# Storing two branch results as high and low parts instead of splitting them at the merge

## The chip, the cores and the metric

The kernel runs on one core of one Trainium2 chip. The metric is device time in microseconds (us); lower is better. A core has five engines with queues of their own: TensorE (PE, with a separate row PEld for its weight loads), VectorE (DVE), ScalarE (ACT), GpSimd (POOL) and SyncE (SP). Here SP issues nearly all transfers (DMAs), one after the other, and each engine takes its instructions strictly in the order in which they stand. An instruction that waits holds up what stands behind it on the same engine.

## The reference, cut to what matters

One layer over 2048 positions of width 1024 (all float32). One input projection feeds three branches: forgetting attention (12 heads of 64), a state-space layer with a gated linear unit (GLU), and an attention into 256 memory tokens (4 heads of 128). The three results are projected, weighed with gates, added, and projected out:

```python
y_s5 = jax.nn.gelu(y_s5)
y_s5 = y_s5 * jax.nn.sigmoid(y_s5 @ w_glu[l] + b_glu[l])
y_s5 = y_s5 * jax.nn.silu(gs)
...
y_mem = memory_attention(...)
y_mem = y_mem * jax.nn.silu(gm)
gates = jax.nn.sigmoid(gl + b_merge[l]).reshape(Bn, L, N_BRANCH, D_MODEL)
merged = (gates[:, :, 0] * (y_fox @ w_proj_fox[l])
          + gates[:, :, 1] * (y_s5 @ w_proj_s5[l])
          + gates[:, :, 2] * (y_mem @ w_proj_mem[l]))
x = x + merged @ w_out[l]
return rms_norm(x, g_final)
```

`y_s5` and `y_fox` are 768 wide (6 tiles of 128 channels), `y_mem` 512 (4 tiles).

## The kernel before, in words

**High and low parts.** A float32 product is made of three passes in the faster format fp32r (`mm3`): each operand x is split into hi = x rounded to fp32r and lo = x - hi, and PE adds hi·hi, hi·lo and lo·hi. `split` makes the parts of a tile that lies in SBUF: hi on POOL (line 893; on ACT, line 891, once `hi_act` is set, unless `pool=True`), lo on DVE (line 895, or 897 with a scale). Where PSUM is the source, ACT makes hi and DVE lo.

**Stages.** (1) Up to about 1550 us the input projection runs tile by tile on PE, and between its chunks, at fixed rates, the side work: `gen_s5` (to about 930 us), `gen_glu` (to about 1185 us) and `gen_mem` (to about 1535 us). (2) Then the forgetting attention (`gen_fox`) runs, and between its steps a filler: first the rest of the gate projection (`gen_gl`), then `gen_merge0`, the merge of the last quarter of the positions (chunk 3 of 4; a chunk is 512 positions, `CW`). `gen_merge0` begins at about 2350 us, and it has a part 0 (branches 1 and 2, results kept in `s_mp`) and a part 1 (branch 0, added to it). (3) `merge_out` merges chunks 2, 1 and 0 and makes the output projection. All intermediate results go through DRAM (`s["ys"]`, `s["ym"]`, `s["yx"]`, ...).

**What is split where.** `gen_glu` and `gen_mem` store `y_s5` and `y_mem` as plain float32: one store of 256 KB per tile of 128 channels x 512 positions (lines 884 and 678). The merge reads 16 tiles per chunk (`SRC`: six of ys, four of ym, six of yx). `merge_load` loads each into a ring `yr` of two buffers, and splits it into a tile `y` (named `ymg`, 128 x 1024: hi in the left half, lo in the right) with `split(..., pool=True)`, so POOL and DVE each have one instruction per tile.

**In the GLU** each step n loads its gate into `gs` (ring of two), DVE multiplies it into `gt` (line 878), ACT writes the tanh over `gs` (line 882), DVE makes the result in `gs` (line 883), and SP stores it. The load of `gs` two steps on waits until that store has landed.

**What sets the order.** The program is written once in Python order; a scheduler then simulates it and writes a fixed order for every engine. A change of a dependency can so move instructions of other work. The names of tiles in the rows below carry running numbers that differ between the two programs.

**Rings of the merge.** `yp` and `yq` hold 16 `ymg` tiles each. `self.over` is set once the attention is through; the merge then uses PSUM tiles `psA` (3) and `psF` (1) by turns, and `merge_out` uses psB (3) for branch 1, psC (1) for branch 2 and psA for branch 0. In `gen_merge0` the gate tiles `g` and the ring `yr` have two buffers each.

Of the kernel before, what the change touches and what calls it, by code (L numbers as in the profile page):

```python
# [4 lines left out]
F32 = mybir.dt.float32  # L5
F32R = mybir.dt.float32r
# [6 lines left out]
D = 1024  # L13
L = 2048
NC = 4
CW = 512
KD = 8
ML = 256
DF = 768
H = 12  # L20
DH = 64
DM = 512
# [23 lines left out]
def fl32(ap):  # L46
    return ap.bitcast(F32)


class Layer:  # L50
# [17 lines left out]
    def setup(self):  # L68
        nc, i = self.nc, self.i
        self.const, self.close_const = self.pool("const", side="right")  # L70
        self.wp, self.close_wp = self.pool("wp", side="right")
        self.ps, self.close_ps = self.pool("ps", space=PSUM)
        c = self.const
        self.eps = c.tile([128, 1], F32, name="eps")
        nc.vector.memset(self.eps, EPS)
        warm = c.tile([128, 1], F32, name="warm")
        nc.scalar.activation(warm, self.eps, AF.Sqrt)
        self.ident = c.tile([128, 128], F32, name="ident")
        nc.scalar.dma_start(out=self.ident, in_=i["ident"])
        self.g1 = c.tile([128, KD], F32, name="g1")  # L80
        nc.scalar.dma_start(out=self.g1, in_=i["g_norm"])
        self.identb = c.tile([128, 128], BF16, name="identb")
        nc.vector.tensor_copy(self.identb, self.ident)
        pw = self.psC()
        for n in range(WARM):
            nc.tensor.matmul(pw[:, :128], self.identb, self.identb, start=True, stop=True)
        s = {}
        for n, sh, dt in (
            ("qh", [DF, L], F32), ("ql", [DF, L], F32), ("kh", [DF, L], F32), ("kl", [DF, L], F32),
            ("vs", [H, 16, 128, 128], F32), ("gf", [DF, L], F32), ("gs", [DF, L], F32),  # L90
            ("gl", [3 * D, L], F32), ("gm", [DM, L], F32), ("qmh", [DM, L], F32), ("qml", [DM, L], F32),
            ("u", [6, 8, 128, 256], F32), ("kd", [48, 16, 128], F32), ("nf", [H, L], F32), ("yx", [DF, L], F32), ("yc", [6, 8, 128, 256], F32),
            ("ys", [DF, L], F32), ("ym", [DM, L], F32), ("mp", [D, CW], F32), ("mg", [D, L], F32),
            ("mkh", [128, HM, ML], F32), ("mkl", [128, HM, ML], F32),
            ("mvh", [128, 2, DM], F32), ("mvl", [128, 2, DM], F32),
        ):
            s[n] = self.dram("s_" + n, sh, dt)
        self.s = s
# [562 lines left out]
    def mem_pv(self, p, hd, j, G, P):  # L661
        nc, s = self.nc, self.s
        po = self.psC()
        cs = slice(G * 512, (G + 1) * 512)
        for kt in range(2):
            ps = self.psB()
            for b in range(4):
                nc.tensor.transpose(ps[:, b * 128:(b + 1) * 128], P[b][:, kt * 128:(kt + 1) * 128], self.ident)
            hi = p.tile([128, 512], F32R, tag="mhi", name="mhi", bufs=1)
            lo = p.tile([128, 512], F32R, tag="mlo", name="mlo", bufs=1)  # L670
            nc.scalar.copy(hi, ps)
            nc.vector.tensor_sub(lo, ps, fl32(hi))
            vs = slice(j * 128, (j + 1) * 128)
            self.mm3(po, (self.mv[0][:, kt, vs], self.mv[1][:, kt, vs]), (hi, lo), kt == 0, kt == 1)
            yield
        gm = hd[2]
        nc.vector.tensor_mul(gm, po, gm)
        nc.sync.dma_start(out=s["ym"][j * 128:(j + 1) * 128, cs], in_=gm)
        yield

    def gen_mem(self):
# [166 lines left out]
    def gen_glu(self):  # L848
        nc, s = self.nc, self.s
        p, close = self.pool("glu", side="right")  # L850
        t = lambda n, dt=F32, bufs=2: p.tile([128, CW], dt, tag=n, name=n, bufs=bufs)
        for c in range(NC):
            cs = slice(c * CW, (c + 1) * CW)
            ys = []
            for k in range(6):
                y = t("gy")
# [3 lines left out]
                h, l = t(f"gh{k}", F32R, 1), t(f"gl{k}", F32R, 1)  # L860
# [10 lines left out]
            for n in range(6):  # L871
                w = self.load_w(self.i["w_glu"][n], (6, 128))
                r = slice(n * 128, (n + 1) * 128)
                gs = t("gs")
# [6 lines left out]
                    self.mm3(ps, (w[0][:, k, :], w[1][:, k, :]), ys[k], k == 0, k == 5)  # L881
                nc.scalar.activation(gs, ps, AF.Tanh, bias=self.bg[:, n:n + 1], scale=0.5)
                nc.vector.scalar_tensor_tensor(out=gs, in0=gs, scalar=1.0, in1=y, op0=ALU.add, op1=ALU.mult)
                nc.sync.dma_start(out=s["ys"][r, cs], in_=gs)
                yield
        close()

    def split(self, hi, lo, x, sc=1.0, pool=False):
# [7 lines left out]
        else:  # L896
            self.nc.vector.scalar_tensor_tensor(out=lo, in0=x, scalar=sc, in1=fl32(hi), op0=ALU.mult, op1=ALU.subtract)

    SRC = [("ys", k, 1) for k in range(6)] + [("ym", k, 2) for k in range(4)] + [("yx", k, 0) for k in range(6)]

    def merge_load(self, c, part, p, rp, bufs=2):

        for n, k, _ in part:
            raw = rp.tile([128, CW], F32, tag="yr", name="yr", bufs=bufs)
            self.nc.sync.dma_start(out=raw, in_=self.s[n][k * 128:(k + 1) * 128, c * CW:(c + 1) * CW])
            y = p.tile([128, 1024], F32R, tag="y", name="ymg", bufs=16)
            self.split(y[:, :CW], y[:, CW:], raw, pool=True)
            self.ys[c].append((y[:, :CW], y[:, CW:]))

    def merge_gate(self, p, br, m, c, bufs=GB):  # L910
# [254 lines left out]
```

## Time and profile before

| | |
|---|---|
| time, median of 3 runs | 3046.73 us (3043.87 to 3050.66) |
| the profiled execution | 3043.67 us, span 3041.6 us |
| PE busy | 2960.3 us (97%) |
| DVE busy | 1858.7 us (61%) |
| ACT busy | 1015.4 us (33%) |
| POOL busy | 899.2 us (30%) |
| moved by DMA | 417.81 MB, mean 137 GB/s |

The span is the time from the first to the last instruction on the core. The difference between 3043.67 and 3041.6 us lies around it. PE is the engine that is nearly always busy, so time is to be found where PE stands idle or where its clock is granted below full (column PEclk). A row of a view by stretches gives, for each stretch of the span, the busy time of PE, PEld, DVE, ACT and POOL with the number of instructions, then PEclk (1.00 is full), the busy share of the 16 DMA engines and the rate. A row of the waits reads "engine line <- whom it waited for: us in total, times, longest".

### The profile page before, as it was taken

The page shows a single profiled execution, that of the slowest core. Times are in us where ns is not written, and L with a number is a line of the kernel's source. Part 1 is how long each engine was busy: PE and PEld are TensorE (multiplying, and loading weights), DVE is VectorE, ACT ScalarE, POOL GpSimd, SP SyncE. Part 2 cuts the span into 40 slices and gives each one's busy share as a digit, 9 for nine tenths or more (in the row PEclk, how much of TensorE's full clock was granted, in tenths as well). Part 3 has the DMA queues.
Part 4 walks back from the last instruction along what each step waited for, and adds up shares of the span by engine and source line. Part 5 has one row for each costly group of instructions (what it writes and reads, how often), then busy time and mean ns, then how long its engine had stood idle before and what let it go on. Part 6 is the DMA issues. An engine that isn't in the chain of part 4 may idle for free.

```text
span 3041.6 us, 43711 instructions
## 1 busy us (share of the span) xinstructions
PE 2960.3 (97%) x14656; PEld 2424.9 (80%) x14656; DVE 1858.7 (61%) x4982; ACT 1015.4 (33%) x1997; POOL 899.2 (30%) x1212
## 2 busy tenths in 40 slices
PE   8999999999999999999999999999999898999999
PEld 7889977777777778888878888888888676778787
DVE  5332399898986673332217777767777885664444
ACT  5102111111112231222216666666666551212222
POOL 0010000000002332122205666665655764432100
PEclk9999999999999999999999999999999998999999
DMA  5343323323335555344352443444444548777542
GB/s 168 108 136 99 102 87 113 121 88 122 118 128 155 173 158 171 119 122 133 118 165 80 122 120 109 133 118 118 126 117 115 149 130 271 223 226 218 173 145 97
DMA packets 306672, 417.81 MB, mean 137 GB/s; under 512 B 84084, under 2 KB 165236, under 8 KB 306436
## 3 DMA queue, kind: packets, MB, share of 16 engines
q1 hardware_dynamic: 306160, 414.95, 45.8%
q8 instruction: 117, 1.92, 0.3%
q14 instruction: 107, 0.88, 0.1%
q10 hardware_dynamic: 288, 0.07, 0.0%
HBM read 276.00 MB, written 138.90 MB: 136 GB/s over the span
## 4 chain that ended last, share of the span: by engine, by line
PE 80%; DMA 8%; DVE 5%; POOL 3%; issue 3%; ACT 1%; SPq 0%; DVEq 0%; POOLq 0%; ACTq 0%
PE psF L147 10%; PE psF L148 10%; PE psF L149 10%; PE psA L149 8%; PE psA L147 8%; PE psA L148 8%; PE psC L799 5%; PE psB L783 5%; PE psA L751 3%; PE psA L752 3%; PE psC L147 2%; PE psC L149 2%; PE psC L148 2%; DMA wraw<-in_w_out 1%; PE psB L147 1%
## 5 line engine op out<-in xcount | busy, mean ns | idle before, releaser
L147 PE MATMUL psF<-hh,whi 128*128 128x512 f32 (+1 forms) x1160 | 468.9, 404 | 6.2 <-ACT ehi L238 3.1
L149 PE MATMUL psF<-hh,wlo 128*128 128x512 f32 (+1 forms) x1160 | 460.0, 397 | 0.2 <-DVE wlo L895 0.2
L148 PE MATMUL psF<-hl,whi 128*128 128x512 f32 (+1 forms) x1160 | 459.6, 396 | 0.0
L893 POOL TENSOR_SCALAR whi<-wraw 128x1024 fp32r<-128x1024 f32 (+2 forms) x132 | 134.3, 1018 | 703.9 <-PE psA L148 308.0
L895 DVE TENSOR_TENSOR wlo<-wraw,whi 128x1024 fp32r<-128x1024 f32 (+2 forms) x168 | 209.6, 1249 | 190.4 <-POOL whi L893 147.9
L147 PE MATMUL psA<-hh,whi 128*128 128x512 f32 (+1 forms) x816 | 321.8, 396 | 2.9 <-POOL whi L893 1.9
L148 PE MATMUL psA<-hl,whi 128*128 128x512 f32 (+1 forms) x816 | 323.2, 396 | 0.0
L149 PE MATMUL psA<-hh,wlo 128*128 128x512 f32 (+1 forms) x816 | 321.1, 394 | 0.6 <-DVE wlo L895 0.6
L799 PE MATMUL psC<-Pt,v 128*128 128x512 f32 x864 | 267.8, 399 | 7.3 <-DVE Pt L787 4.0
L787 DVE TENSOR_TENSOR Pt<-psB,Pt 128x512 fp32r<-128x512 f32 x336 | 225.5, 684 | 72.9 <-ACT Pt L786 70.7
L147 PEld LDWEIGHTS psF<-hh,whi 128*128 128x128 f32 x1160 | 218.9, 189 | 53.0 <-ACT ehi L238 3.5
L149 PEld LDWEIGHTS psF<-hh,wlo 128*128 128x128 f32 x1160 | 218.8, 189 | 51.5 <-DVE wlo L895 0.6
L148 PEld LDWEIGHTS psF<-hl,whi 128*128 128x128 f32 x1160 | 219.2, 189 | 45.9 <-issue 0.4
L753 DVE CUSTOM_DVE_ANT_0 P<-psA,nf 128x512 f32<-128x512 f32 (+1 forms) x336 | 201.1, 626 | 46.4 <-PE psA L752 27.0
L786 ACT CAST Pt<-psB 128x512 fp32r<-128x512 f32 x336 | 191.6, 586 | 98.8 <-PE psB L783 53.4
L762 POOL TENSOR_SCALAR P<-P,rd 128x768 f32<-128x768 f32 (+1 forms) x240 | 193.8, 823 | 57.4 <-DVE rd L759 34.2
L751 PE MATMUL psA<-kk,qh 128*128 128x512 f32 (+1 forms) x480 | 184.7, 391 | 8.0 <-DVE mx L753 3.9
L147 PEld LDWEIGHTS psA<-hh,whi 128*128 128x128 f32 x816 | 153.6, 189 | 38.3 <-POOL whi L893 2.9
L799 PEld LDWEIGHTS psC<-Pt,v 128*128 128x128 f32 x864 | 154.1, 190 | 35.4 <-DVE Pt L787 7.1
L149 PEld LDWEIGHTS psA<-hh,wlo 128*128 128x128 f32 x816 | 154.0, 189 | 35.5 <-DVE wlo L895 0.8
L783 PE MATMUL psB<-ident,P 128*128 128x128 f32 x1200 | 176.4, 273 | 5.7 <-DVE Pt L787 5.6
L148 PEld LDWEIGHTS psA<-hl,whi 128*128 128x128 f32 x816 | 154.0, 189 | 33.6 <-DVE hl L188 0.2
(372 smaller groups left out, 6259.1 us busy)
## 6 DMA issues: line engine op xcount, KB each, us to landing
wraw<-in_w_in SPq DMA_DIRECT2D x90, 512.0 KB, 4.3
s_gl<-ehi SPq DMA_DIRECT2D x96, 256.0 KB, 2.6
g<-s_gl SPq DMA_DIRECT2D x96, 256.0 KB, 5.0
wraw<-in_w_proj SPq DMA_DIRECT2D x40, 320.0 KB, 4.4
s_vs<-ev_v SPq DMA_DIRECT2D x48, 256.0 KB, 2.7
nf<-s_nf SPq DMA_DIRECT2D x24, 512.0 KB, 6.6
v<-s_vs SPq DMA_DIRECT2D x24, 512.0 KB, 6.8
qh<-s_qh SPq DMA_DIRECT2D x96, 128.0 KB, 3.9
```

Of the source, the lines that this page charges most:

```text
L147: nc.tensor.matmul(out, a[0], b[0], start=first, stop=False)
L148: nc.tensor.matmul(out, a[0], b[1], start=False, stop=False)
L149: nc.tensor.matmul(out, a[1], b[0], start=False, stop=last)
L751: nc.tensor.matmul(ps[:, :wm], q[0][:, qs], kk[:, c0:c0 + wm], start=True, stop=False)
L753: nc.vector.tensor_tensor_reduce(out=pr[:, c * 512:c * 512 + w], in0=ps[:, :w], in1=nf[:, c0:c0 + w], scale=1.0, scalar=-3.0e38, op0=ALU.a ...
L762: nc.gpsimd.tensor_scalar(out=c, in0=c, scalar1=rd, scalar2=0.5, op0=ALU.mult, op1=ALU.mult)
L783: nc.tensor.transpose(ps[:, o:o + 128], P[b][:, kt * 128:(kt + 1) * 128], self.ident)
L786: nc.scalar.copy(hi, psv)
L787: nc.vector.tensor_sub(lo, psv, fl32(hi))
L799: self.pe = nc.tensor.matmul(o, v, m, start=(kt == 0), stop=(kt == 2 * G + 1))
L893: self.nc.gpsimd.tensor_scalar(out=hi, in0=x, scalar1=sc, scalar2=1.0, op0=ALU.mult, op1=ALU.mult)
L895: self.nc.vector.tensor_sub(lo, x, fl32(hi))
```

## The change

`gen_glu` and `gen_mem` split their results where they are made, and store both parts; `merge_load` loads the two parts of ys and ym straight into the halves of the `ymg` tile. The results of the forgetting attention (yx) are stored, loaded and split as before.

```diff
-            ("ys", [DF, L], F32), ("ym", [DM, L], F32), ...
+            ("ysh", [DF, L], F32), ("ysl", [DF, L], F32), ("ymh", [DM, L], F32), ("yml", [DM, L], F32), ...
@@ mem_pv
         nc.vector.tensor_mul(gm, po, gm)
-        nc.sync.dma_start(out=s["ym"][j * 128:(j + 1) * 128, cs], in_=gm)
+        self.keep(p.tile([128, 512], F32R, tag="mgh", name="mgh", bufs=2), gm, "ym", slice(j * 128, (j + 1) * 128), cs)
@@ gen_glu
                 nc.vector.scalar_tensor_tensor(out=gs, in0=gs, scalar=1.0, in1=y, op0=ALU.add, op1=ALU.mult)
-                nc.sync.dma_start(out=s["ys"][r, cs], in_=gs)
+                self.keep(t("gsh", F32R), gs, "ys", r, cs)
@@
+    def keep(self, hi, x, n, r, cs):
+        nc, s = self.nc, self.s
+        lo = x.bitcast(F32R)
+        nc.scalar.copy(hi, x)
+        nc.vector.tensor_sub(lo, x, fl32(hi))
+        nc.sync.dma_start(out=s[n + "h"][r, cs], in_=fl32(hi))
+        nc.sync.dma_start(out=s[n + "l"][r, cs], in_=x)
@@ merge_load
         for n, k, _ in part:
-            raw = rp.tile([128, CW], F32, tag="yr", name="yr", bufs=bufs)
-            self.nc.sync.dma_start(out=raw, in_=self.s[n][k * 128:(k + 1) * 128, c * CW:(c + 1) * CW])
+            r, cs = slice(k * 128, (k + 1) * 128), slice(c * CW, (c + 1) * CW)
             y = p.tile([128, 1024], F32R, tag="y", name="ymg", bufs=16)
-            self.split(y[:, :CW], y[:, CW:], raw, pool=True)
+            if n == "yx":
+                raw = rp.tile([128, CW], F32, tag="yr", name="yr", bufs=bufs)
+                self.nc.sync.dma_start(out=raw, in_=self.s[n][r, cs])
+                self.split(y[:, :CW], y[:, CW:], raw, pool=True)
+            else:
+                self.nc.sync.dma_start(out=fl32(y[:, :CW]), in_=self.s[n + "h"][r, cs])
+                self.nc.sync.dma_start(out=fl32(y[:, CW:]), in_=self.s[n + "l"][r, cs])
```

**SP where `gen_merge0` begins (chunk 3).** Before, two loads of `yr` go out, and the others stand behind other transfers, each pair waiting for the splits:

```order
L727 DMA ql_24457<-s_ql_118 64x512
L905 DMA yr_24021<-s_ys_133 128x512
L905 DMA yr_24026<-s_ys_133 128x512
L912 DMA g_24367<-s_gl_124 128x512
L808 DMA s_yx_131<-oo_23816 64x256
L773 DMA gf_24004<-s_gf_122 64x256
L727 DMA ql_24457<-s_ql_118 64x512
L912 DMA g_24528<-s_gl_124 128x512
L139 DMA wraw_24629<-in_w_proj 128x640
L905 DMA yr_24031<-s_ys_133 128x512
```

In the changed program (the same place; `ql` is a low part of the queries of the attention, loaded in two halves):

```order
L727 DMA ql_24599<-s_ql_118 64x512
L920 DMA ymg_24183<-s_ysh_133 128x512
L921 DMA ymg_24183<-s_ysl_134 128x512
L920 DMA ymg_24186<-s_ysh_133 128x512
L808 DMA s_yx_131<-oo_23978 64x256
L773 DMA gf_24166<-s_gf_122 64x256
L921 DMA ymg_24186<-s_ysl_134 128x512
L920 DMA ymg_24189<-s_ysh_133 128x512
L921 DMA ymg_24189<-s_ysl_134 128x512
L920 DMA ymg_24192<-s_ysh_133 128x512
L921 DMA ymg_24192<-s_ysl_134 128x512
```

All 20 loads of chunk 3 now stand nearly in one run (12 more of them follow these rows), and the second half of `ql` stands behind them.

**PE where `gen_merge0` ends and chunk 2 begins.** Before, the last rows of branch 0 (psA with `hix`, `lox`) are followed by branch 1 of chunk 2 for two output tiles at once (psB_26391 and psB_26481), input tile by input tile (the number of `ymg`):

```order
L148 MATMUL psA_26571<-ymg_26387,hix_26588 128x512
L149 MATMUL psA_26571<-ymg_26387,lox_26589 128x512
L147 MATMUL psB_26391<-ymg_26304,whi_26395 128x512
L147 MATMUL psB_26481<-ymg_26304,whi_26485 128x512
L148 MATMUL psB_26391<-ymg_26304,whi_26395 128x512
L149 MATMUL psB_26391<-ymg_26304,wlo_26396 128x512
L148 MATMUL psB_26481<-ymg_26304,whi_26485 128x512
L149 MATMUL psB_26481<-ymg_26304,wlo_26486 128x512
L147 MATMUL psB_26391<-ymg_26309,whi_26395 128x512
L147 MATMUL psB_26481<-ymg_26309,whi_26485 128x512
```

In the changed program, branch 2 of chunk 2 (psC_26514, twelve matmuls, the first five of them in these rows) stands already between two blocks of part 1 of chunk 3 (psF_26259 and, behind the twelve, psA_26355), some 130 matmuls before branch 1 of chunk 2:

```order
L148 MATMUL psF_26259<-ymg_26183,whi_26253 128x512
L149 MATMUL psF_26259<-ymg_26183,wlo_26254 128x512
L147 MATMUL psC_26514<-ymg_26462,hib_26523 128x512
L148 MATMUL psC_26514<-ymg_26462,hib_26523 128x512
L149 MATMUL psC_26514<-ymg_26462,lob_26524 128x512
L147 MATMUL psC_26514<-ymg_26465,hib_26523 128x512
L148 MATMUL psC_26514<-ymg_26465,hib_26523 128x512
```

The inputs of chunk 2 so have to be there earlier, and the blocks of two output tiles are no longer mixed.

**DVE in the GLU.** Before (`wlo` is the low part of a weight, `elo` that of an input projection):

```order
L895 TENSOR_TENSOR wlo<-wraw,whi 128x1024
L883 SCALAR_TENSOR_TENSOR gs<-gs,gt 128x512
L878 SCALAR_TENSOR_TENSOR gt<-gt,gs 128x512
L895 TENSOR_TENSOR wlo<-wraw,whi 128x768
L883 SCALAR_TENSOR_TENSOR gs<-gs,gt 128x512
```

In the changed program:

```order
L895 TENSOR_TENSOR wlo<-wraw,whi 128x1024
L883 SCALAR_TENSOR_TENSOR gs<-gs,gt 128x512
L904 TENSOR_TENSOR gs<-gs,gsh 128x512
L878 SCALAR_TENSOR_TENSOR gt<-gt,gs 128x512
L895 TENSOR_TENSOR wlo<-wraw,whi 128x768
L883 SCALAR_TENSOR_TENSOR gs<-gs,gt 128x512
```

Line 904 is the new subtraction; it stands right behind line 883, and waits for ACT's copy of the same tile.

More of the change, by code (lines that the diff above doesn't have):

```diff
@@ L92, in setup @@
             ("u", [6, 8, 128, 256], F32), ("kd", [48, 16, 128], F32), ("nf", [H, L], F32), ("yx", [DF, L], F32), ("yc", [6, 8, 128, 256], F32),
-            ("ys", [DF, L], F32), ("ym", [DM, L], F32), ("mp", [D, CW], F32), ("mg", [D, L], F32),
+            ("ysh", [DF, L], F32), ("ysl", [DF, L], F32), ("ymh", [DM, L], F32), ("yml", [DM, L], F32), ("mp", [D, CW], F32), ("mg", [D, L], F32),
             ("mkh", [128, HM, ML], F32), ("mkl", [128, HM, ML], F32),
```

## The prediction

> **What bounds the kernel now.** First the page: its busy times and the clock in 40 slices.
>
> ```profile
> span 3041.6 us, 43711 instructions
> PE 2960.3 (97%) x14656; PEld 2424.9 (80%) x14656; DVE 1858.7 (61%) x4982; ACT 1015.4 (33%) x1997; POOL 899.2 (30%) x1212
> PEclk9999999999999999999999999999999998999999
> ```
>
> PE is the bound. It is idle for 3041.6 - 2960.3 = 81.3 us, and the change touches no matmul, so it can only win or lose in that idle time and in the slow clock that follows it. Next the view by stretches, at the places that the change touches:
>
> ```profile
> core 0: us, PE busy (x) PEld busy (x) DVE busy (x) ACT busy (x) POOL busy (x), PEclk, DMA share, GB/s
> 940.00:1200.00 260.00, 249.32 (x1042) 196.67 (x1041) 160.66 (x200) 68.84 (x97) 89.44 (x82) 0.98 0.59 174
> 1200.00:1500.00 300.00, 300.00 (x1438) 248.02 (x1437) 88.59 (x190) 78.80 (x191) 59.83 (x137) 1.00 0.42 122
> 1550.00:1560.00 10.00, 6.90 (x24) 5.17 (x23) 1.23 (x1) 1.31 (x2) 1.48 (x2) 0.83 0.86 267
> 2350.00:2376.00 26.00, 19.13 (x90) 14.46 (x89) 20.44 (x43) 12.23 (x24) 17.74 (x23) 0.87 0.60 186
> 2508.00:2626.00 118.00, 98.61 (x388) 75.60 (x387) 69.30 (x78) 21.39 (x29) 52.99 (x52) 0.93 0.76 245
> 2626.00:2690.00 64.00, 64.00 (x279) 52.12 (x279) 40.01 (x47) 13.74 (x18) 24.41 (x24) 1.00 0.81 244
> 2690.00:2704.00 14.00, 11.28 (x43) 8.72 (x42) 8.54 (x12) 2.21 (x3) 5.50 (x7) 0.88 0.67 211
> 2500.00:2580.00 80.00, 67.09 (x272) 52.34 (x271) 44.87 (x55) 17.12 (x28) 32.71 (x33) 0.93 0.80 265
> 2540.00:2550.00 10.00, 8.25 (x28) 6.20 (x29) 6.05 (x7) 3.27 (x4) 3.07 (x4) 0.83 1.01 384
> ```
>
> I count a stretch's loss as PE's idle time plus (1 - PEclk) times its busy time. Where the merge of chunk 3 begins (2350 to 2376): 6.9 + 0.13 x 19.1 = 9.4 us. Where it passes into chunk 2 (2508 to 2626): 19.4 + 0.07 x 98.6 = 26.3 us. At the start of the attention (1550 to 1560): 3.1 + 0.17 x 6.9 = 4.3 us. Where chunk 2 passes into chunk 1 (2690 to 2704): 2.7 + 0.12 x 11.3 = 4.1 us. In the memory attention (1200 to 1500) PE never waits. Then, who makes PE wait (first block: 2350 to 2376; second: 2508 to 2626):
>
> ```profile
> PE psB L783 <- DVE Pt L787: 4.7, 2, 2.4
> PE psA L751 <- DVE mx L753: 0.9, 1, 0.9
> ...
> PE psB L147 <- POOL ymg L893: 6.8, 3, 4.9
> PE psF L147 <- DVE g L960: 3.5, 1, 3.5
> PE psA L147 <- ACT whi L891: 3.3, 2, 2.6
> PE psC L147 <- DVE g L1000: 2.3, 2, 1.5
> PE psA L147 <- ACT hix L891: 1.6, 1, 1.6
> PE psC L147 <- POOL ymg L893: 0.7, 1, 0.7
> ```
>
> In the second block the splits (`ymg`) are named themselves. In the first DVE is named, for work of the attention; the order of time shows what stands in front of that work:
>
> ```profile
> 2367.64 1.38 DVE L895 TENSOR_TENSOR ymg<-yr,ymg 128x512 fp32r<-128x512 f32 x1 [1.28 <-POOL ymg L893]
> 2368.94 1.27 DVE L787 TENSOR_TENSOR Pt<-psB,Pt 128x512 fp32r<-128x512 f32 x2
> ...
> 2369.67 1.26 PE L783 MATMUL psB<-ident,P 128*128 128x128 f32 x8 [2.42 <-DVE Pt L787]
> ```
>
> DVE sits idle for 1.28 us behind a split whose hi part POOL has not made, subtracts for 1.38 us, and only then makes the `Pt` for which PE has waited 2.42 us.
>
> **The change part by part.** The instructions:
>
> ```profile
> L893 POOL TENSOR_SCALAR ymg<-yr x64: 608/622/1331, 2357.3 to 2702.3; 128x512 fp32r<-128x512 f32 x64
> L895 DVE TENSOR_TENSOR ymg<-yr,ymg x64: 674/693/2577, 2357.9 to 2703.6; 128x512 fp32r<-128x512 f32 x64
> L905 SPq DMA_DIRECT2D yr<-s_ys x24: 319/320/476, 2353.4 to 2669.3; - x24
> ...
> L147 PE MATMUL psF<-ymg,whi x96: 391/394/767, 2376.3 to 2564.8; 128*128 128x512 f32 x96
> ...
> L671 ACT CAST mhi<-psB x32: 586/587/589, 1210.1 to 1523.7; 128x512 fp32r<-128x512 f32 x32
> ```
>
> Of 64 splits 40 go: 40 x 0.62 = 25 us of POOL and 40 x 0.69 = 28 us of DVE, all after 2350 us. 40 copies on ACT (0.59 each by the nearest row, 24 us) and 40 subtractions on DVE (28 us) come in before 1540 us. 40 stores and 40 loads of 256 KB are added, each 10.5 MB.
>
> *A, start of the merge.* The splits in 2350 to 2376 go, and with them the waits of DVE on POOL. What stays is the attention's own chain. I take 7 of the 9.4 us. Against it: the 20 loads (5.24 MB) go out in one run, and at the 384 GB/s of the busiest 10 us above they need 13.7 us, at 265 / 0.80 = 331 GB/s 15.8 us. The half of `ql` that stands behind them is used shortly after the first merge matmuls, which came 2376.3 - 2353.4 = 23 us after the first load; less the 7 won that is 16 us, and landing takes some 4 us more than moving. So it is just covered, or up to 4 us late. Bounds -9.4 and +4.
>
> *B, chunk 3 into chunk 2.* The splits' own waits (6.8 + 0.7), and those from the mixed order of two tiles that the late splits forced (2.3 and 1.6 us), make 11.4 us; the slow clock goes with them in proportion, 6.9 x 11.4 / 19.4 = 4.1 us. I take -15. The waits on `g` and on the weights (3.5 + 3.3) hang on transfers and stay. Bounds -20 (the psC blocks that now stand between part 1's cover some of those too) and 0 (see the third rival).
>
> *G, the transfers there.* In 2500 to 2580 the chip moved 265 x 80 = 21.2 MB. By the order the added loads of chunk 2 and of chunk 1, 2.62 MB each, fall into or next to this stretch: 26.4 MB. At 384 GB/s that is 68.8 us, against 67.1 us of PE work, at 331 GB/s 79.8 us. Where chunk 0's loads come (around 2690), 2.62 MB more at 244 / 0.81 = 301 GB/s are 8.7 us in a stretch that was busy for 81% and already lost 4.1 us. Bounds: -4 (the splits' part of that) and +21 (12.7 + 8.7). I take +4: the loads are not needed at once, and the order gives most of them 10 us and more.
>
> *C, the GLU.* In each step DVE and the store come later. The loop of `gs`:
>
> ```profile
> L882 ACT ACTIVATE gs<-psC,bg x24: 668/689/695, 967.5 to 1179.6; 128x512 f32<-128x512 f32 x24
> gs<-s_gs SPq DMA_DIRECT2D x24, 256.0 KB, 4.1
> s_ys<-gs SPq DMA_DIRECT2D x24, 256.0 KB, 4.1
> s_kh<-ehi SPq DMA_DIRECT2D x24, 256.0 KB, 2.6
> s_kl<-elo SPq DMA_DIRECT2D x24, 256.0 KB, 3.5
> ...
> 1032.34 0.68 DVE L883 SCALAR_TENSOR_TENSOR gs<-gs,gt 128x512 f32<-128x512 f32 x1
> 1043.98 0.69 DVE L878 SCALAR_TENSOR_TENSOR gt<-gt,gs 128x512 f32<-128x512 f32 x1 [3.96 <-DMA gs<-s_gs]
> 1045.47 0.69 DVE L883 SCALAR_TENSOR_TENSOR gs<-gs,gt 128x512 f32<-128x512 f32 x1
> ```
>
> From one step to the one two later takes 1045.47 - 1032.34 = 13.1 us. PE has for two steps 36 matmuls and one chunk of the projection, 24: at 64.00 / 279 = 0.23 us each 13.8 us. The change adds 0.59 (copy) + 0.69 (subtraction) + about 0.9 (the second of two stores, as s_kl against s_kh) = 2.2 us, so 15.3 us, 1.5 over PE's 13.8. There are three pairs of steps per chunk and four chunks: 12 x 1.5 = 18 us if nothing absorbs it. Two PSUM buffers and the GELU part between the chunks do absorb some; but behind line 878 DVE holds `wlo` and `elo`, for which PE waits. In the GELU parts DVE gains some three subtractions per passage, 3 x 3 x 0.69 = 6.2 us, where it is nearly full. Bounds 0 and +18; I take +5, nearer to the first, as the waiting PE had 249.3 of 260 us busy here and the loop lags at most 4.5 us per chunk.
>
> *D, start of the attention.* PE waited here for a tile `ehi` whose store stood on SP behind the attention's loads:
>
> ```profile
> 1555.21 0.50 PE L147 MATMUL psF<-hh,whi 128*128 128x512 f32 x1 [3.10 <-ACT ehi L238]
> ...
> 1590.05 0.50 PE psA L751
> ```
>
> The changed order puts one of the two stores ahead of these loads, which themselves come some 2 us later (they wait for the last `s_yml`); PE needs them at 1590. I take -4 of the 4.3 us. Bounds -4.3 and +2.
>
> *F, the memory attention.* 16 copies and 16 subtractions beside a PE that never waits, with DVE busy 88.6 of 300 us: nothing; if a psC were freed later, 16 x 0.69 would be 11 us, but the subtraction reads no PSUM.
>
> SP issues 80 more transfers at 0.32 us each, 26 us in 3041, beside its waits. Sum: A -7, B -15, G +4, C +5, D -4, F 0: -17 us, 3043.67 - 17 = 3026.7 in the profiled execution. The median of the runs is 3.06 us above it, so 3046.7 - 17 = 3029.7: I predict 3030 us.
>
> **The rivals.** *First, slower: the doubled loads make the merge transfer-bound.* Place: the three runs of loads, at 2350, 2505 to 2580, and 2690. For it: DMA share 0.76 to 1.01 there, and PE's waits on `g` and weights, which are transfers. Against it: the loads lie ahead of their use. Price: +12.7 and +8.7 (from G) and about +8 where `ql` comes late, 29 instead of G's +4: 3030 + 25 = 3055. It decides from the point where the three cost more than 21 + 6 us. The Trainium skill, "DMA: Bandwidth & Descriptors", section "Specifications", puts the limit of a core's HBM traffic at about 358 GB/s. The trace's 384 GB/s over 10 us is above that, so I do not take the figure as a ceiling. By it the 26.4 MB would need 73.7 us, an estimate from that page, 6.6 us over PE's 67.1.
>
> *Second: the GLU loop decides.* C at its +18 instead of +5: 3043, no change. For it: the 1.5 us over; against it: what absorbs the lag.
>
> *Third: the waits in B only change their name.* PE would wait for the loads of chunk 2, or for `g`, where it waited for the splits: B 0 instead of -15, 3045, no change. For it: part 1 is held by transfers already (3.5 + 3.3 us). Against it: chunk 2's loads now start before part 1.
>
> **How the numbers follow.** The forecast has 0.70, the first rival 0.13, the second 0.08, the third 0.09. 0.2% is 6 us, about what a measurement of this kernel can tell from no change: 3040.6 and 3052.8 are the borders. The second and third lie inside, though half of the second reaches below; a part of the first too. Faster 0.71, same 0.16, slower 0.13. The forecast's own range takes A -9.4, B -20, G 0, C +2, D -4 as its low end: -31, 3015; and G +8, C +9, A -4 as its high: -6, 3041. For 8 in 10 it must reach to the second and third rival, with the runs' own spread of some 3 us: 3015 to 3050.
>
> **What would show it.** A: PE idle in the 23 us behind the first `ymg` load falls from 6.9 to under 2 us, with no `ymg` row of DVE among the Pt rows. B: no PE wait on `ymg` L893 of branch 1 or 2, and PEclk back near 1.0 at the passage. G: DMA share at 0.9 and more for tens of us, and PE's waits named `g`, `whi` or a DMA. C: in 940 to 1200 PE idle rises from 10.7 to about 15 us; if it rises by more than 15, the loop was the bound. D: the 3.1 us at 1555 gone. The prediction is wrong if the order's early loads starve the attention or part 1, which would show as PE waits on `qh`, `ql` or `g` of over 5 us each.

## Result and profile after

The changed kernel takes 3015.86 us (median of 4 runs, 3014.89 to 3018.25), beside 3045.30 us of the kernel before in the same comparison. The ratio is 0.9904, with a 95% interval of 0.9892 to 0.9916: 29 us, or 1.0%, faster. Predicted were 3030 us and a range of 3015 to 3050. The sign held; the gain is 12 us larger than the forecast, and the time lies less than 1 us inside the low end of the range. The profiled execution of the changed kernel took 3014.89 us. Its page:

```profile
span 3013.1 us, 43815 instructions
...
PE 2952.8 (98%) x14656; PEld 2417.1 (80%) x14656; DVE 1855.6 (62%) x4982; ACT 1038.5 (34%) x2037; POOL 881.0 (29%) x1172
...
PEclk9999999999999999999999999999999999999999
...
DMA packets 318195, 438.80 MB, mean 146 GB/s; under 512 B 85365, under 2 KB 166517, under 8 KB 317957
```

PE has the same 14656 matmuls. It is idle for 3013.1 - 2952.8 = 60.3 us instead of 81.3, and the slice in which the clock had fallen to 8 tenths is gone. 21 MB more are moved.

Where the time went is read best from four instructions that stand in both programs in the same order: the last result of the memory attention (line 677), the first score of the forgetting attention (line 751), its last PV matmul (line 799), and the first matmul of the output projection (`psF<-wo`). The view by source line ends each row with the first and the last start. Before:

```profile
L677 DVE TENSOR_TENSOR mgm<-psC,mgm x16: 683/692/693, 1223.6 to 1530.2; 128x512 f32<-128x512 f32 x16
...
L751 PE MATMUL psA<-kk,qh x480: 274/393/793, 1590.0 to 2493.8; 128*128 128x512 f32 x113, 128*128 128x256 f32 x31, 128*128 128x384 f32 x16
...
L799 PE MATMUL psC<-Pt,v x864: 274/393/796, 1613.1 to 2512.0; 128*128 128x512 f32 x154, 128*128 128x256 f32 x19
...
L147 PE MATMUL psF<-wo,whi x128: 390/393/404, 2855.2 to 3027.7; 128*128 128x512 f32 x128
```

After:

```profile
L677 DVE TENSOR_TENSOR mgm<-psC,mgm x16: 683/692/693, 1230.8 to 1535.6; 128x512 f32<-128x512 f32 x16
...
L751 PE MATMUL psA<-kk,qh x480: 274/393/505, 1590.6 to 2484.4; 128*128 128x512 f32 x113, 128*128 128x256 f32 x31, 128*128 128x384 f32 x16
...
L799 PE MATMUL psC<-Pt,v x864: 274/393/767, 1613.6 to 2502.6; 128*128 128x512 f32 x154, 128*128 128x256 f32 x19
...
L147 PE MATMUL psF<-wo,whi x128: 390/393/404, 2826.7 to 2999.2; 128*128 128x512 f32 x128
```

From the output projection on, both take 186.4 us (3041.6 - 2855.2 and 3013.1 - 2826.7). So the 28.5 us lie in four stretches. They are measured in the same way for every kernel below, each in its one profiled execution; the first is counted from the last matmul of the state-space layer (line 626, which starts for the last time between 925.4 and 929.2 us in all of them):

| kernel | median, us | ratio to before | to line 677 | to line 751 | to line 799 | to `wo` |
|---|---|---|---|---|---|---|
| before | 3045.3 | 1 | 604.5 | 59.8 | 922.0 | 343.2 |
| changed | 3015.9 | 0.9904 (0.9892 to 0.9916) | 608.1 | 55.0 | 912.0 | 324.1 |
| e1: splits in place | 3023.1 | 0.9934 (0.9921 to 0.9948) | 604.0 | 61.9 | 922.1 | 322.8 |
| e2: in place, loaded twice | 3032.0 | 0.9967 (0.9954 to 0.9979) | 604.0 | 62.1 | 922.6 | 325.9 |
| e3: only ys kept in parts | 3035.2 | 0.9977 (0.9967 to 0.9987) | 608.6 | 60.5 | 913.6 | 335.0 |
| e4: only ym kept in parts | 3039.0 | 0.9986 (0.9976 to 0.9997) | 604.6 | 54.6 | 923.2 | 343.9 |
| e5: no split in the GLU | 3015.9 | 0.9909 (0.9893 to 0.9925) | 608.6 | 54.7 | 913.1 | 323.6 |
| e6: `gs` ring of three | 3014.3 | 0.9903 (0.9888 to 0.9917) | 605.9 | 54.7 | 912.2 | 325.1 |
| e9: parts for the last quarter | 3020.7 | 0.9919 (0.9903 to 0.9936) | 604.8 | 58.9 | 909.8 | 325.6 |
| e10: e9, and yx in place | 3024.7 | 0.9939 (0.9924 to 0.9955) | 604.7 | 58.9 | 912.7 | 330.6 |
| e11: ys, ym loads on POOL | 3043.2 | 1.0006 (0.9997 to 1.0015) | 604.4 | 60.6 | 921.1 | 343.7 |
| e12: split on POOL alone | 3027.9 | 0.9957 (0.9944 to 0.9971) | 604.7 | 58.9 | 924.0 | 324.3 |
| e13: e12, and ym in parts | 3021.0 | 0.9926 (0.9914 to 0.9939) | 604.5 | 54.7 | 923.7 | 323.8 |
| e14: the whole ring on POOL | 3058.8 | 1.0055 (1.0042 to 1.0068) | 605.1 | 61.2 | 921.9 | 354.2 |

(The names are those of the experiments below. Medians of different comparisons shift with the median of the kernel before, 3040.7 to 3045.3 us; the ratios take this out.) The first three columns fall into clear groups: a stretch that an edit does not touch repeats within about 1 us in the first column and within 3 to 4 us in the next two. In the fourth, e3 and e10 lie between the groups. The changed kernel's sum is then: first stretch +3.6, second -4.8, third -10.0, fourth -19.1, and +1.8 from before line 626, where both programs compute the same.

The views by stretches of the changed kernel, for the rows that the prediction showed of the kernel before:

```profile
core 0: us, PE busy (x) PEld busy (x) DVE busy (x) ACT busy (x) POOL busy (x), PEclk, DMA share, GB/s
2346.00:2370.00 24.00, 20.40 (x107) 15.88 (x106) 16.59 (x42) 14.80 (x32) 13.15 (x20) 0.93 0.97 316
2498.00:2616.00 118.00, 107.46 (x442) 83.99 (x441) 62.40 (x71) 25.48 (x35) 42.40 (x36) 0.96 0.96 331
2510.00:2570.00 60.00, 51.72 (x203) 39.18 (x203) 22.92 (x27) 10.48 (x13) 12.03 (x12) 0.92 1.02 357
2616.00:2680.00 64.00, 64.00 (x279) 52.17 (x278) 32.85 (x42) 13.12 (x17) 25.23 (x18) 1.00 0.86 290
940.00:1207.00 267.00, 252.82 (x1058) 197.88 (x1057) 189.26 (x225) 82.93 (x120) 94.43 (x80) 0.99 0.62 190
1550.00:1560.00 10.00, 10.00 (x45) 8.05 (x44) 1.23 (x1) 0.69 (x1) 1.48 (x2) 1.00 1.08 217
```

At the passage from chunk 3 to chunk 2 (now 2498 to 2616) the loss by the prediction's count is 10.5 + 0.04 x 107.5 = 14.8 us instead of 26.3. DMA runs at a share of 1.02 and 357 GB/s for 60 us there. What PE waits for at the passage now:

```profile
PE psC L147 <- ACT hib L891: 6.0, 2, 5.3
PE psF L147 <- DVE g L974: 2.3, 1, 2.3
PE psA L147 <- ACT whi L891: 1.4, 2, 0.7
PE psC L149 <- DVE lob L895: 0.6, 2, 0.4
PE psA L149 <- DVE wlo L895: 0.3, 1, 0.3
```

No row names `ymg`. The largest is a weight (`hib`), and the order of time shows the transfer in it (SP issues the load `raw`, ACT splits it, PE uses it):

```profile
2536.07 0.33 SPq L938 DMA_DIRECT2D raw<-in_w_proj  x1
...
2541.89 0.74 ACT L891 ACTIVATE hib<-raw 128x640 fp32r<-128x640 f32 x1 [1.21 <-DMA raw<-in_w_proj]
...
2542.68 0.80 PE L147 MATMUL psC<-ymg,hib 128*128 128x512 f32 x1 [5.25 <-ACT hib L891]
```

5.8 us pass from the issue to ACT's start. Loads of this kind took no less before: their median from issue to landing is 6.1 us in 2508 to 2626 of the kernel before and 5.8 in 2498 to 2616 of the changed one (for the loads of yx the median rose from 3.0 to 5.7). The 20 loads of ys and ym for chunk 2 had gone out by 2522, and those for chunk 1 begin at 2548. So PE does wait for a transfer here, for about 6 us, but for one that was asked for 1.4 us before PE came to it; that the added loads made this wait is not shown. The splits' waits that went were larger.

### The profile page after: what moved, and what is told of

The parts are those of the page before. It is cut to its first block, busy times and chain, and to the rows that moved or that the text cites. A ratio compares the mean times of both kernels' runs of the same rounds, so it can differ in the third digit from the quotient of the medians.

```text
span 3013.1 us, 43815 instructions
## 1 busy us (share of the span) xinstructions
PE 2952.8 (98%) x14656; PEld 2417.1 (80%) x14656; DVE 1855.6 (62%) x4982; ACT 1038.5 (34%) x2037; POOL 881.0 (29%) x1172
## 4 chain that ended last, share of the span: by engine, by line
PE 52%; DMA 5%; DVE 2%; POOL 1%; issue 1%; ACT 1%; SPq 0%; DVEq 0%; POOLq 0%; ACTq 0%
PE psF L147 6%; PE psF L148 6%; PE psF L149 6%; PE psC L799 5%; PE psB L783 5%; PE psA L147 4%; PE psA L149 4%; PE psA L148 4%; PE psA L752 3%; PE psA L751 3%; PE psB L147 1%; PE psB L148 1%; PE psB L149 1%; PE psC L147 1%; PE psC L149 1%
```

## The experiments

Two theories of the fourth stretch's 19 us were tried first. *Theory 1*: the two buffers of `yr` make SP stand still, and all that stands behind on SP comes late. *Theory 2*: the split instructions on POOL and DVE are what PE waits for.

**e1, splits in place.** The plain ys and ym are loaded straight into the lo half of `ymg`, and split there.

```diff
-            raw = rp.tile([128, CW], F32, tag="yr", name="yr", bufs=bufs)
-            self.nc.sync.dma_start(out=raw, in_=self.s[n][...])
             y = p.tile([128, 1024], F32R, tag="y", name="ymg", bufs=16)
+            raw = rp.tile(... "yr" ...) if n == "yx" else fl32(y[:, CW:])
+            self.nc.sync.dma_start(out=raw, in_=self.s[n][...])
             self.split(y[:, :CW], y[:, CW:], raw, pool=True)
```

> The kernel before, with ys and ym stored plain as before, but loaded straight into the lo half of the ymg tile and split there in place (hi by POOL into the left half, lo by DVE over the raw data). The ring yr of two buffers no longer holds these 40 loads back on SP; no transfer is added, every split stays at the merge, the GLU and the memory attention are those of before. Theory 1 (the splits cost because two buffers of yr made SP stand still behind each pair, and with it all that lay behind on SP): nearly the whole gain of the merge comes, A -6 to -8 and the passage from chunk 3 to chunk 2 with what follows -15 to -19, in all -20 to -27: 3018 to 3026 us. Theory 2 (the instructions themselves, POOL's hi and DVE's lo among the attention's DVE work, are what PE waits for): A stays, psB L783 <- DVE Pt keeps its 4.7 us, ymg L893 its 7.5 us; at most -8 in all: 3037 to 3046 us. The start of the attention at 1555 keeps its 3.1 us by both.

Measured: 0.9934, 20 us faster. All of it is in the fourth stretch, 343.2 to 322.8 us, without one split or transfer less. The third stays at 922.1. PE's waits in the first 55 us of the merge (2345 to 2400) still name the attention's work behind the splits:

```profile
PE psB L783 <- DVE Pt L787: 5.2, 2, 2.8
PE psB L783 <- DVE Pt L792: 2.2, 1, 2.2
PE psC L799 <- DVE ot L803: 2.1, 1, 2.1
PE psA L751 <- DVE mx L753: 1.1, 1, 1.1
```

So the two places have different causes: at the passage the ring, with what its removal moves, and beside the attention the split work itself. Theory 1 foretold the time in all, but also 6 to 8 us in the third stretch, and those did not come. The order that the scheduler wrote for e1 also takes chunk 2's branch 1 for one output tile at a time, as in the changed kernel.

**e2, the same, loaded twice.**

```diff
             self.nc.sync.dma_start(out=raw, in_=src)
+            if n != "yx":
+                self.nc.sync.dma_start(out=fl32(y[:, :CW]), in_=src)
```

> As the kernel with the splits in place, and each ys and ym tile loaded twice (256 KB more into the hi half, which POOL then overwrites; the second load is of no use). So the merge has the transfers of the changed kernel and the split work of the kernel before. Against the kernel with the splits in place it gives the price of the 40 added loads (10.5 MB) alone: my prediction's G says +4 us (bounds -4 to +21); if transfers are the limit where the clock of the queues shows a share near 1.0, +10 to +20; theory 1, with the loads asked for early, says 0 to +4. Against the changed kernel it gives the price of the split work with all else alike in the merge: theory 1 says 0 to 5 us, theory 2 10 to 20 us.

Measured: 9 us more than e1 by the medians (3032.0 against 3023.1), 10 by the ratios, 3.1 us by the fourth stretch of the two profiles (the profiled run of e1 was the longest of its five, that of e2 among the shortest). The added 10.5 MB so cost 3 to 10 us here, which does not decide between the prediction's +4 and the +10 of a merge limited by transfers. In the changed kernel no split waits for the added loads, and no run prices them there. The changed kernel is 19 us (0.6%) faster than e2 by the ratios, and 14.5 by the two profiled runs: 10.6 of these are the stretch with the splits beside the attention, 7.1 the start of the attention, 1.8 the fourth stretch, and -4.1 the GLU (the rest lies before line 626). The whole difference is what theory 2 foretold (10 to 20 us), but less than two thirds of it lie beside the attention, and hardly any at the passage.

**e3 and e4, one of the two results alone.** e3 leaves `ym` as before, e4 leaves `ys`; each is the store line and the name tested in `merge_load`.

```diff
# e3
-        self.keep(p.tile(... "mgh" ...), gm, "ym", ...)
+        nc.sync.dma_start(out=s["ym"][...], in_=gm)
-            if n == "yx":
+            if n != "ys":
# e4
-                self.keep(t("gsh", F32R), gs, "ys", r, cs)
+                nc.sync.dma_start(out=s["ys"][r, cs], in_=gs)
-            if n == "yx":
+            if n != "ym":
```

> The changed kernel, but y_mem is stored, loaded and split as before; only ys is kept as high and low parts. GLU as in the changed kernel (+3.6 us by the marker of the last memory-attention instruction). Of 40 splits 24 are gone, and with them 60% of the loads that wait for the ring. If the gain of the merge goes by the number of splits: 0.6 x 27 = -16, with the GLU +3.6 and the start of the attention as before (0): about 3035 us. By theory 1 the four tiles of ym still hold SP twice per chunk, behind the ys loads: most of the gain, -18 to -22, stays: 3027 to 3031 us. The start of the attention (3.1 us at 1555) should be back, since the stores of the memory attention are those of before.

> The changed kernel, but the GLU stores y_s5 plain, and the merge loads and splits it as before; only y_mem is kept as high and low parts. The GLU is then that of before: the marker of the last memory-attention instruction (1530 before, 1536 in the changed kernel) goes back by 3 to 4 us. The start of the attention keeps the gain (-4 to -5 us). By the number of splits the merge gains 0.4 x 27 = -11, by theory 1 little (0 to -6), since ys is the first that is loaded, the ring still holds SP, and the mixed order of two tiles in chunk 2 is still there. In all 3028 us by the number of splits, 3034 to 3041 us by theory 1.

Measured: e3 3035.2 us, e4 3039.0 us. The columns separate cleanly: the GLU's cost goes with ys (608.6 against 604.6), the start of the attention with ym (54.6 against 60.5), the attention's gain with ys (913.6 against 923.2). The passage does not add: ys alone gives 8.2 of 19.1 us, ym alone nothing. While one of the two still goes through the ring of two buffers, most of that gain is not there. Neither theory foretold both: e3 came out where the number of splits put it (3035), e4 where theory 1 did (3034 to 3041).

**e5 and e6, the GLU.** e5 leaves out ACT's copy and DVE's subtraction in the GLU and stores the plain result twice, so that its merge computes with twice y_s5; e6 gives `gs` a third buffer.

```diff
# e5
-                self.keep(t("gsh", F32R), gs, "ys", r, cs)
+                nc.sync.dma_start(out=s["ysh"][r, cs], in_=gs)
+                nc.sync.dma_start(out=s["ysl"][r, cs], in_=gs)
# e6
-                gs = t("gs")
+                gs = t("gs", F32, 3)
```

> The changed kernel, but the GLU leaves out ACT's copy and DVE's subtraction, and stores the plain result to both places (so the merge computes with twice y_s5). Two stores per step stay. The marker of the last memory-attention instruction stands at 1535.6 in the changed kernel and at 1530.7 to 1531.7 where the GLU is that of before. If the arithmetic is what C costs (subtractions of 1.24 us in front of the wlo for which PE waits): back to about 1531, -4 to -5 us, 3011 us. If the longer loop of gs is (copy and subtraction are 1.3 of its 2.2 us, the second store 0.9): -2 to -3 us. If the second store is: 0.

> The changed kernel with a ring of three buffers for gs in the GLU instead of two. If C is the loop of gs (load of the gate waits for the store of two steps earlier), as the prediction worked it out, the loop goes away and the marker at 1535.6 falls by 3 to 5 us: 3011 to 3013 us. If C is DVE's added work in front of wlo, nothing moves: 3016 us.

Measured: without the arithmetic the first stretch stays at 608.6, so the copy and the subtraction cost nothing that can be told from the 1 us by which this stretch repeats. With the third buffer it falls to 605.9, 1.4 us over the kernel before: 2.2 of the 3.6 us hang on the ring of `gs`, less than the 3 to 5 foretold. That leaves the second store in that loop, or what waits for it, as C's cause; no run takes one store away. In whole runs neither can be told from the changed kernel (0.9909 and 0.9903 against 0.9904).

**e9 and e10, towards a better version.** Parts are kept only for chunk 3, which is merged beside the attention; chunks 2, 1 and 0 are stored plain and split in place. e10 loads yx in place too.

```diff
-                self.keep(t("gsh", F32R), gs, "ys", r, cs)
+                if c == NC - 1: self.keep(...)          # the same for ym
+                else: nc.sync.dma_start(out=s["ysh"][r, cs], in_=gs)
@@ merge_load
+            elif c < NC - 1:
+                raw = fl32(y[:, CW:])
+                self.nc.sync.dma_start(out=raw, in_=self.s[n + "h"][r, cs])
+                self.split(y[:, :CW], y[:, CW:], raw, pool=True)
# e10: for yx as well
-                raw = rp.tile([128, CW], F32, tag="yr", name="yr", bufs=bufs)
+                raw = fl32(y[:, CW:])
```

> y_s5 and y_mem are kept as high and low parts for the last quarter of the positions alone (chunk 3, which is merged beside the attention); for the other three quarters they are stored plain, loaded once into the lo half of the ymg tile and split there. By the parts as the runs so far have them: GLU +1 to +2 instead of +4 to +5, the start of the attention -5 if it goes by the stores of the last chunk (0 otherwise), the attention with the merge beside it -10 as in the changed kernel, the passage and what follows -20 as with the splits in place, and no doubled loads there. Sum -33 to -34: 3009 us in the scale where the kernel before has 3042. If the parts do not add (the splits of chunk 2 fall beside the end of the attention, or the doubled loads cost nothing there): 3014 to 3020.

> As the kernel that keeps the last quarter alone, and yx too is loaded into the lo half of the ymg tile and split there, so that the ring yr holds only the part sums. If SP still stands still for yx behind the two buffers (six tiles per chunk), another -2 to -6 us: 3004 to 3007. If the changed kernel's loads are already early enough: the same within 2 us.

Measured: 3020.7 and 3024.7 us. e10 is behind the changed kernel; e9's interval overlaps with that of the changed kernel, but it is not the gain that was hoped for. e9's stretches come out about as expected (604.8, 909.8, 325.6), but for the start of the attention: 58.9; the 55 are there only in the kernels that keep ym in parts for all chunks. Its profiled run, 3012.9, was the shortest of five that reach to 3024; the changed kernel's four lie within 3.4 us. Loading yx in place, which was to win 2 to 6 us or nothing, lost 5 us in the fourth stretch, by a cause that is not known. So freeing the ring further is no gain by itself.

**e11 and e14, the ring stays, its loads leave SP.** The kernel before, with the loads issued by POOL's queue: ys and ym in e11; every load into the ring, also yx and the part sums `s_mp`, in e14.

```diff
-            self.nc.sync.dma_start(out=raw, in_=self.s[n][...])
+            q = self.nc.sync if n == "yx" else self.nc.gpsimd     # e14: gpsimd for all
+            q.dma_start(out=raw, in_=self.s[n][...])
```

> The kernel before, with one thing changed: the loads of ys and ym into the ring yr (two buffers, as before) are issued by POOL's queue instead of SP's. So the ring still makes the splits late, and PE's order still has branch 1 of chunk 2 for two output tiles at once, but SP no longer stands still for it, and the gates and weights behind are asked for in time. The stretch from the attention's last PV matmul to the first output projection is 343 us in the kernel before, 323 to 326 us in the kernel with the splits in place and in the changed kernel. If the held SP is the cause: 323 to 330 us, in all 3022 to 3030 us. If the late splits and the order they force are the cause: 338 to 345 us, in all 3037 to 3045. The attention beside the merge stays at 922 us by both (POOL now also waits for buffers, which could add some us there).

> In the kernel whose ys and ym loads went to POOL's queue, the yx loads stayed on SP and stood there for buffers of the same ring: SP was held for 26 us (12.4 + 10.0 + 2.8 + 0.9) at the passage, against 30 us (25.5 + 2.7 + 1.0 + 0.6 + 0.5) in the kernel before, so that run did not free SP. Here every load into the ring yr (ys, ym, yx and the part sums) is issued by POOL's queue; nothing on SP waits for the ring. PE's order still has branch 1 of chunk 2 for two output tiles at once. If the held SP is the cause of the 19 us: the stretch from the last PV matmul to the first output projection falls from 343 to 323 to 332 us, in all 3022 to 3032 us. If the late splits (each tile's load waits until the tile two places ahead is split) and the order that goes with them are the cause: 338 to 346 us, PE's waits on ymg L893 stay at 7 to 10 us, in all 3037 to 3046 us.

Measured: e11 343.7 us in the fourth stretch and 3043.2 in all, no gain. But its waits of SP's queue at the passage (2500 to 2630) show that SP was not free; the loads of yx stood there for the same ring:

```profile
SPq L906 <- DVE ymg L895: 12.4, 7, 5.3
SPq L906 <- DMA yr<-s_ym: 10.0, 1, 10.0
```

The kernel before has, in the same window:

```profile
SPq L905 <- DVE ymg L895: 25.5, 25, 2.9
```

e14 takes those loads off SP as well. There nothing on SP waits for the ring, and the stretch became 11 us longer, 354.2, outside what either theory expected; in all 3058.8 us. The wait for the ring now holds POOL, which also makes the sums of the gates and the hi parts (waits of POOL, 2500 to 2640):

```profile
POOL yr L905 <- DVE ymg L895: 23.1, 15, 5.2
```

Neither run bears out theory 1 as put, that it is SP's standing still that costs. They do not refute it either: in e11 SP still stood, and in e14 POOL stood in its place, while SP waited longer for other work (50.9 us for `wlo` in 2500 to 2630, 12.0 in the kernel before). What the runs support is the ring itself. A load may go out only when the tile two places ahead has been split, whichever engine issues it; in 2500 to 2630 of the kernel before, this chain of load, POOL, DVE, load held SP for the 25.5 us above, and it goes away with the ring (e1) and with the splits (the changed kernel). Whether its 19 us come through the late tiles, the held queue or the order of PE's instructions that came with it, no run separates. The kernel before, e4, e11 and e14 take two output tiles at once, e1 and the changed kernel one. The order alone does not give the 19 us: e3 too takes one tile at a time, and it has 8.2 us of them.

**e12 and e13, the split beside the attention on POOL alone.** e1, with the low part of ys and ym in chunk 3 on POOL too, so that DVE has none of them; e13 also keeps ym in parts.

```diff
+            if n != "yx" and c == NC - 1:
+                self.nc.gpsimd.tensor_scalar(out=y[:, :CW], in0=raw, ...)
+                self.nc.gpsimd.tensor_sub(y[:, CW:], raw, fl32(y[:, :CW]))
+            else:
                 self.split(y[:, :CW], y[:, CW:], raw, pool=True)
```

> The kernel with the splits in place, and in the last quarter (the merge beside the attention) the ten splits of ys and ym are made by POOL alone, the low part too, so that DVE has none of them and never waits for POOL there. From the attention's first score to its last PV it takes 922 us in the kernels that split ys on both engines there, 910 to 914 us in those that load ready parts. If DVE, held behind POOL's hi part with the attention's Pt behind it, is the cause (the prediction's A): 911 to 916 us, in all 3013 to 3017 us. If the splits cost because POOL works beside DVE at all: 918 to 924 us, in all 3020 to 3025 us, as before this edit.

> As the kernel whose last quarter is split on POOL alone, and y_mem kept as high and low parts in all quarters as in the changed kernel; y_s5 is stored plain. By the parts: GLU 0, start of the attention -5 (59.8 to 55 us from the last memory-attention instruction to the first score, as in the kernel that keeps ym alone), attention -7 to -10 if the split on POOL alone costs nothing, passage -18 to -20. Sum -30 to -35 from 3043: 3008 to 3013 us, which would be below the changed kernel. If the split on POOL does not help: 3016 to 3020.

Measured: the third stretch stays at 924.0 and 923.7, and in all the two are 3 and 1 us above even the higher of their expectations. PE's largest wait there is new; its order of time, then POOL's and its row by line in e12:

```profile
2376.49 2.90 PE L799 MATMUL psC<-Pt,v 128*128 128x512 f32 x6 [10.38 <-DVE ot L803]
```

```profile
2372.74 1.29 POOL L913 TENSOR_TENSOR ymg<-ymg 128x512 fp32r<-128x512 f32 x1
2373.98 0.82 POOL L762 TENSOR_SCALAR P<-P,rd 128x640 f32<-128x640 f32 x1
2374.75 0.74 POOL L806 TENSOR_TENSOR oo<-oo,ot 64x256 f32<-64x256 f32 x1
```

```profile
L913 POOL TENSOR_TENSOR ymg<-ymg x10: 1283/1290/1306, 2357.8 to 2380.3; 128x512 fp32r<-128x512 f32 x10
```

Ten times 0.63 + 1.29 us lie in POOL's queue from 2357 to 2380, and the attention's own steps on POOL (`P` by `rd`, `oo` with `ot`) stand between and behind them. `ot` has one buffer: ACT begins the next one at 2375.52, right behind POOL's line 806 that reads the `ot` before it, and DVE makes the `ot` for which PE waits at 2375.92. DVE was relieved and POOL now holds the attention.

PE's second wait there, 5.35 us, has another path. It is for `Pt`, which DVE makes at 2384.02, behind a split of yx that still is DVE's:

```profile
2377.34 6.76 DVE L895 TENSOR_TENSOR ymg<-yr,ymg 128x512 fp32r<-128x512 f32 x2 [0.99 <-POOL ymg L893]
2384.02 1.87 DVE L787 TENSOR_TENSOR Pt<-psB,Pt 128x512 fp32r<-128x512 f32 x3
```

```profile
2376.66 1.23 POOL L893 TENSOR_SCALAR ymg<-yr 128x512 fp32r<-128x512 f32 x2
2377.83 3.75 POOL L913 TENSOR_TENSOR ymg<-ymg 128x512 fp32r<-128x512 f32 x3
2381.51 0.74 POOL L807 TENSOR_TENSOR oo<-oo,gf 64x256 f32<-64x256 f32 x1
2382.20 0.74 POOL L806 TENSOR_TENSOR oo<-oo,ot 64x256 f32<-64x256 f32 x1
```

The first of the two subtractions took 6.16 us, the longest of the row of its line (679/814/6156 ns), and ended 0.56 us behind POOL's unbroken work. So the split work on POOL also made DVE slow. Whether DVE alone was the cause is not shown; that this place has no engine with room for ten splits is (e1, e12, e13: 922 to 924), and that they must go from it (changed, e3, e9: 910 to 914).

## Why the prediction was right, and what was mis-sized

- **A, start of the merge** (-7 taken, bounds -9.4 and +4): the third stretch gained 10.0 us. By e3 and e4 it belongs to ys and its splits; by e1 it is the split work, as the prediction said. Only 4.4 us lie where A looked for 7 (from the first load of the merge to its first matmul 22.9 us before, 2370.4 - 2351.9 = 18.5 after). 3.5 lie behind, and 2.1 ahead of the first load, where neither kernel splits for the merge: that part is no work of A's mechanism, and the 10.0 exceed A's bound only with it. The sign named for it was too sharp: PE is idle for 3.6 us there, not under 2, behind `Pt` and `ot` that now wait for ACT. The late second half of `ql` cost 2.6 us of waits in the whole attention, inside the bound of 4.
- **B and G, the passage and its transfers** (-15 and +4, together -11): -19.1 in the fourth stretch. This is the term that was mis-sized, but not at the passage. There -26.3 + 14.8 = -11.5 is what the two gave together. In e1, which adds no transfers, the passage (first row below) loses 7.5 + 0.03 x 110.5 = 10.8 us, 15.5 less than before: B's -15; and the changed kernel's 14.8 is 4.0 more: G's +4, though e1's passage also still has its splits. What the sum lacked lies behind the passage, where the prediction looked for a price of chunk 0's loads. There the changed kernel has no loss at all up to 2680 (PE busy for 64.00 of 64 us at 1.00), so the 4.1 us at 2690 were won, which stood only as G's lower bound. PE's wait of 2.7 us there was for a gate product that DVE made right behind a split, which had waited 1.28 us for POOL: the path that the prediction had drawn for A. About 3 us more were won from there to the output projection (4.85 + 0.02 x 146.4 = 7.8 us before, 3.4 + 0.01 x 143.3 = 4.9 after, by the last two rows). In e1 the whole fourth stretch is -20.4, and by the two stretches the added transfers are a net +1.3, by e2 +3 to +10. The passage in e1:

```profile
2511.00:2629.00 118.00, 110.47 (x463) 87.88 (x462) 79.30 (x94) 25.85 (x35) 65.14 (x57) 0.97 0.89 295
```

From chunk 1 to the output projection, before and after:

```profile
2704.00:2855.20 151.20, 146.35 (x625) 118.75 (x624) 77.93 (x96) 36.33 (x52) 47.01 (x28) 0.98 0.68 209
```

```profile
2680.00:2826.70 146.70, 143.27 (x615) 116.31 (x615) 69.24 (x89) 35.73 (x51) 44.89 (x26) 0.99 0.66 201
```

- **C, the GLU** (+5): PE's idle time in 940 to 1207 is 267.00 - 252.82 = 14.2 us, 10.7 before, near the 15 foretold. The first `mgm` of line 677 comes 1230.8 - 1223.6 = 7.2 us later, 5.4 without the 1.8 from before. Right in size; but by e5 the copy and the subtraction, 1.3 of the 2.2 us per step, were no part of it that can be told, so the size owes something to luck.
- **D, start of the attention** (-4): the 3.1 us at 1555 are gone, -4.8, and by e4 and e13 the gain is ym's: PE's wait for `ehi` there is gone in them, and is 2.2 to 4.3 us in e1, e2, e3, e9 and e12. F (0): the memory attention is 1.8 us shorter from its first to its last `mgm`.
- **First rival**, a transfer-bound merge. Its sign was there, DMA at 1.02 of its share and 357 GB/s for 60 us, a 5.25 us wait for a weight, whose load took no longer than its like before; its price was not, +3 to +10 us by e2 instead of 29. That most loads stand well ahead of their use fits this, but was not varied. The Trainium skill, "DMA: Bandwidth & Descriptors", section "Specifications", puts a core's HBM limit at about 358 GB/s. The 357 of these 60 us lie at that figure, but 10 us before the change ran at 384, so by the traces it is no ceiling here. **Second rival**, the GLU loop at +18: no, +5.4. **Third**, waits that only change their name: in place of 7.5 us for `ymg` stand 6.0 for `hib`, but of the rest (mixed tiles, clock, later chunks) most did not come back. The waits for `qh`, `ql` or `g` of over 5 us each, which would have shown the prediction wrong, are not there.

## What to carry to other kernels

A small ring between a load and a short step on another engine can make a chain, and the place for the loaded data is often in the tile that the step writes: loading into one half of the output tile gave 20 of the 29 us (e1) with no work less. Moving such a ring, or the step, to another queue (e11, e12, e14) moved the wait with it here. Before costing added transfers by bandwidth, ask how far ahead of use they stand: with a DMA share of 0.96 over 60 us (2510 to 2570 of e2), 10.5 MB more of loads cost 3 to 10 us there, where bytes by bandwidth had given 21 (G's upper bound).

## What the runs showed of the hardware

The subtraction of 128x512 that the change adds took two very different times, in the GLU and in the memory attention:

```profile
L904 DVE TENSOR_TENSOR gs<-gs,gsh x24: 676/1236/1778, 973.8 to 1187.3; 128x512 fp32r<-128x512 f32 x24
L904 DVE TENSOR_TENSOR mgm<-mgm,mgh x16: 691/693/695, 1232.2 to 1537.0; 128x512 fp32r<-128x512 f32 x16
```

1.24 us in the median where POOL is busy for a third of the time (94.43 of 267 us), 0.69 in the quieter stretch: the prediction's price of 0.69 from the merge was too low for the GLU, though nothing hung on it. The same shows in the splits of e1 beside the attention, 2354 to 2376:

```profile
L893 POOL TENSOR_SCALAR ymg<-ymg x10: 617/898/1046, 2361.1 to 2370.7; 128x512 fp32r<-128x512 f32 x10
L895 DVE TENSOR_TENSOR ymg<-ymg x10: 786/1014/1320, 2361.8 to 2373.1; 128x512 fp32r<-128x512 f32 x10
```

Both are slower than the 0.62 and 0.69 us of the medians before. What the slow ones have in common is POOL at work beside them. Of the changed kernel's 64 subtractions of this shape (line 904 and the splits of yx) 26 have no POOL instruction beside them, and they all take 0.68 to 0.70 us; the other 38 take up to 3.1 us, 1.23 in the median. The longest of all is e12's 6.16 us, through all but the last 0.56 of which POOL works without a break. The Trainium skill, "SBUF — State Buffer", section "SBUF: two separate sides", has a port pair that POOL and a DVE instruction with two SBUF inputs take by turns, as a lock; the rows agree with that, but no run here changes the inputs alone to show that it is this lock. In these rows a split shared by the two engines costs more than its two parts apart.
